# Three order ties in a two-layer diffusion block: a weight sum behind an output add, a cast behind a copy, two subtractions behind a low part

## The chip, the cores and the metric

The kernel runs on one core of one Trainium2 chip. The metric is the device time of one execution in microseconds (us). A core has five engines with instruction queues of their own: TensorE (PE in the profile, with its weight loads shown apart as PEld), VectorE (DVE), ScalarE (ACT), GpSimd (POOL) and SyncE (SP), which here issues most of the loads.

## The reference

Two layers over 512 latent tokens and 256 context tokens of width 1024, batch 1. Layer 0 is windowed attention, layer 1 is retention in both directions; each is followed by a SwiGLU feed-forward of inner width 2816. Only the latent stream is returned. What matters here is layer 1:

```python
def swiglu(h, w_in, w_out):
    gate, up = jnp.split(h @ w_in, 2, axis=-1)
    return (jax.nn.silu(gate) * up) @ w_out

# bidir_retention, 4 heads of 256 (q, k) and 512 (v, g)
q_x, k_x, v_x, g_x = jnp.split(h_x @ w_qkvg, [qk, 2 * qk, 2 * qk + RET_VWIDTH], axis=-1)
ox_f, _ = retention_chunked(q_x, k_x, v_x, log_g[0], state_f)
ox_b, _ = retention_chunked(flip(q_x), flip(k_x), flip(v_x), log_g[1], state_b)
out_x = (jax.nn.silu(g_x) * normed(ox_f + flip(ox_b))) @ w_o

x = x + mx[2] * out_x
x = x + mx[5] * swiglu(modulate(rms_norm(x, norm2_g), mx[3], mx[4]), ffn_w_in, ffn_w_out)
```

All of it is float32.

## The kernel before

**Three products for one.** A float32 operand is split into a rounded high part and the low part that is left: `split` (L164, L165) makes the high part with a cast on ACT and the low part with a subtraction on DVE. A product is then three matmuls: high by high, low by high, high by low (`mm3`, L147 to L149). Each weight tile of 128 x 1024 is loaded by SP into a raw buffer (`w_raw`, L122), split, and used by PE; the raw buffer is loaded again when its low part is done.

**Seven products for eight.** Most projections use Strassen's scheme on quarters of weights and tokens: sums of weight quarters are formed on DVE ahead of the casts, and PE does seven quarter products. The sums accumulate in PSUM, and intermediate sums are copied out by ACT while PE goes on adding to the same bank.

**The retention heads** (loop `for hd in range(RH)`, heads 0 to 3). For value and gate, DVE forms the weight sums `g12` (L1449) and `v11` (L1450), splits `v11` into `w2` (L1451), splits `g12` into `w3`, and, in heads 1 to 3, subtracts `v11` from `v21` (L1456) and splits the result into `w4`. PE uses `w2`, then `w3`, then `w4`, always adding to the banks `Yv` (shown as tile Z); between them ACT copies the sums into `gate` (L1478, L1481). While this goes on, DVE also does the rotary products of the key (`rope_pair`, L1301 to L1303), whose results ACT and DVE split (tiles qk) for the scores.

**The second feed-forward.** The inner width is 22 tiles of 128, in groups of 2, 4, 4, 4, 4, 4. Tiles f = 0 to 2 are plain projections, f = 3 and later use seven products (`seven`, L1727). In each such tile, `quarter_sums` forms four sums in place (L903 to L906): the third, L905, needs the first, L903, and the fourth needs the third. The gate weight and the up weight, as sums, are cast into `b14` and `b32`. PE then does the products Y, Z, Y, X, Y, Z, Y; the third one's running sum is copied out by ACT at L1746, and the fifth product adds to the same bank after that. `output` (L1773) multiplies a finished group with the output weights into two PSUM banks in turn (tile pj), and DVE adds each of the eight output tiles to the residual (`gated_add`, L256). The output of the first group is written in the program after tile f = 2 and ahead of tile f = 3; `first_adds` holds its first two adds. `copies` holds the copies of L1744 and L1746 of the tile before.

**What sets the order.** The program is written in one order; a planner then makes the queue of each engine. It keeps a clock with its own costs, and gives an engine the earliest instruction of the program that is ready by that clock, so that later work can be put ahead of earlier work that isn't ready yet. Data dependences become semaphores. `after(ins, others)` adds an order tie without a semaphore: the planner may not place `ins` before `others`. Each engine then executes its queue in that order.

Of the kernel before, what the change touches and what calls it, by code (L numbers as in the profile page):

```python
# [49 lines left out]
def dit_kernel(ctx, tc, xT, cT, crow, small, consts, masks, tabs0, tabs1, jtab, adaQ, adaN, adaT, wst, out):  # L50
    nc = tc.nc
    mult, add, sub = ALU.mult, ALU.add, ALU.subtract
# [9 lines left out]
    def T(pool, cols, tag, bufs, dt=F32):  # L62
        return pool.tile([P, cols], dt, tag=tag, bufs=bufs, name=tag)
# [27 lines left out]
    def after(ins, others):  # L91
        for o in others:
            tc.add_manual_dep(ins.ins, o.ins.name, order, reason="table set turn")
# [26 lines left out]
    def w_raw(pool=None, bufs=2):  # L120
        raw = T(pool or rp, 1024, "wraw", bufs)
        nc.sync.dma_start(raw, wst[wpos[0]])  # L122
        wpos[0] += 1
        return raw

    def w_parts(pool, own=2):

        bufs = own
        if ring:
            pool, bufs = ring[wsel[0] % len(ring)], 2  # L130
        elif wsel[0] % (2 + own) < 2:
            pool, bufs = rp, 2
        wsel[0] += 1
        return T(pool, 1024, "whi", bufs, F32R), T(pool, 1024, "wlo", bufs, F32R)
# [28 lines left out]
    def split(t, hi, lo, behind=()):  # L163
        after(nc.scalar.copy(hi, t), behind)  # L164
        return nc.vector.tensor_tensor(lo, t, hi, op=sub)  # L165
# [19 lines left out]
    def t_sq(n):  # L185
        return T(rp, 512, "sq", 2)[:, :n]

    def t_hn(n):
        return T(rp, 512, "hn", 2)[:, :n]
# [644 lines left out]
    late = [context[0], latent[0], context[1], latent[1], latent[2], latent[3]]  # L834
# [62 lines left out]
                nc.tensor.matmul(o, p, r, start=first and k + i == 0, stop=k == 3 and i == 2,  # L897
                                 skip_group_check=not first)

    def quarter_sums(g, u, behind=()):  # L900

        l_, r_ = slice(0, 512), slice(512, 1024)
        after(nc.vector.tensor_tensor(g[:, l_], u[:, l_], g[:, l_], op=sub), behind)  # L903
        nc.vector.tensor_tensor(u[:, l_], u[:, r_], u[:, l_], op=sub)
        nc.vector.tensor_tensor(u[:, r_], u[:, r_], g[:, l_], op=sub)  # L905
        nc.vector.tensor_tensor(g[:, r_], g[:, r_], u[:, r_], op=sub)  # L906

    for s in range(2):
# [236 lines left out]
    f, prev = 0, None  # L1145
# [56 lines left out]
    def chunk(i, own=False):  # L1202
        raw = T(qw, 1024, "wx", 4) if own else T(rp, 1024, "wraw", 2)
        nc.sync.dma_start(raw, wst[i])
        return raw

    def split_chunk(raw, behind=()):
        w = w_parts(hpool[0])
        last_split[0] = split(raw, *w, behind)
        return w  # L1210

    last_split, rope_end, rope_sum, hm, other_sums = [None], [None], [None], [], []
# [83 lines left out]
    def rope_pair(o, cos1, sin1, behind=()):  # L1296

        res = []
        for op, f0, f1 in ((sub, cos1, sin1), (add, sin1, cos1)):
            a, b = t_hn(SX), t_sq(SX)  # L1300
            after(nc.vector.tensor_tensor(a, o[0], f0, op=mult), behind)  # L1301
            after(nc.vector.tensor_tensor(b, o[1], f1, op=mult), behind)
            rope_sum[0] = nc.vector.tensor_tensor(a, a, b, op=op)  # L1303
            hi, lo = t_qk(), t_qk()
            rope_end[0] = split(a, hi, lo)
            res.append((hi, lo))
        return res
# [54 lines left out]
    for hd in range(RH):  # L1362
# [28 lines left out]
        for e, o in halves(Y):  # L1391
            nc.scalar.copy(kt[e][:, HALVES[0]], o)
        product_q(X, quarter_of("12"), k21, True)
        later = [nc.vector.tensor_tensor(kt[e][:, HALVES[0]], kt[e][:, HALVES[0]], o, op=add)
                 for e, o in halves(X)]
# [48 lines left out]
        v11 = []  # L1444
        for i in range(2):
# [4 lines left out]
            nc.vector.tensor_tensor(v11[i], g12[i], v11[i], op=add)  # L1450
            w2.append(split_chunk(v11[i]))  # L1451
        if hd:
            w3 = [split_chunk(g) for g in g12]
            for i in range(2):
                v21 = chunk(bv + 2 + i, True)
                nc.vector.tensor_tensor(v21, v21, v11[i], op=sub)  # L1456
                w4.append(split_chunk(v21))
        else:

            ready, w3, lows = last_split[:], [], []  # L1460
            for g in g12:
                w3.append(split_chunk(g))
                lows += last_split
            for i in range(2):
                nc.scalar.activation(v11[i], v11[i], AF.Identity, scale=-1.0)
                nc.gpsimd.dma_start(v11[i], wst[bv + 2 + i], accum_op=add)
            qh = rope_pair(qt, cos1, sin1, ready)
            for low in lows:
                after(low, rope_sum)
# [65 lines left out]
        for i in range(2):  # L1535
            g, v = chunk(bg + i), chunk(bv + i)
# [140 lines left out]
    norm_end, first_end, first_mult, first_adds = [], [], [], []  # L1677
# [49 lines left out]
    def seven(late=()):  # L1727
        g, u = w_raw(fp, 2), w_raw()
        b11 = w_parts(fp, 4)
        b22 = T(hM, 512, "hm", 8, F32R), T(hM, 512, "hm", 8, F32R)  # L1730
        b14, b32 = w_parts(fp, 4), w_parts(fp, 4)
        split(g, *b11, norm_end)
        split(u[:, 512:1024], *b22, norm_end)
        quarter_sums(g, u, first_end[1:2])
        split(u, *b32, first_adds)
        after(split(g, *b14, first_adds), late)
        X, Y, Z = (T(psF, 512, n, 2)[:, 0:SC] for n in "XYZ")
        t, up = t_hn(SX), t_sq(SX)
        e1, e2 = T(rp, 512, "res", 12), T(rp, 512, "res", 12)
        p1, z1, u2, u3 = e1[:, HALVES[0]], e1[:, HALVES[1]], e2[:, HALVES[0]], e2[:, HALVES[1]]  # L1740
        product(Y, operand_a("11"), b11, 0, True)
        act_parts([nc.scalar.copy(p1, Y)])
        product(Z, operand_a(1), b14, 0, True)
        copies[:] = [nc.scalar.copy(z1, Z)]  # L1744
        product(Y, operand_a(2), b32, 512, False)
        copies.append(nc.scalar.copy(u2, Y))  # L1746
        product(X, operand_a("12"), b11, 512, True)
        nc.vector.tensor_tensor(t[:, HALVES[0]], p1, X, op=add)
        silu(t[:, HALVES[0]], t[:, HALVES[0]])
        product(Y, operand_a(3), b32, 0, False)  # L1750
        nc.scalar.copy(u3, Y)
        product(Z, operand_a(4), b22, 0, False)
        nc.vector.tensor_tensor(up[:, HALVES[0]], u2, Z, op=add)
        product(Y, operand_a("22"), b14, 512, False)
        nc.vector.tensor_tensor(up[:, HALVES[1]], u3, z1, op=add)
        silu(t[:, HALVES[1]], Y)
        nc.vector.tensor_tensor(t, t, up, op=mult)
        act = new_act()
        pending.append((t, *act))
        return act  # L1760

    pending, copies, late = [], [], ()

    def act_parts(behind=()):
        ends = []
        while pending:
            t, hi, lo = pending.pop()
            ends.append(nc.scalar.copy(hi, t))
            after(ends[0], behind)
            ends.append(nc.vector.tensor_tensor(lo, t, hi, op=sub))  # L1770
        return ends
# [23 lines left out]
    f, prev = 0, None  # L1795
    for gsz in FFN_GROUPS:
        acts = []
        for i in range(gsz):
# [9 lines left out]
            late = output(prev, False) if i == 0 and prev is not None else ()  # L1808
# [148 lines left out]
```

## Time and profile before

| what | value |
| --- | --- |
| time, median of 3 runs | 1736.23 us (1734.84 to 1737.31) |
| the profiled execution | 1732.25 us |
| its span, first to last instruction | 1730.3 us |
| granted TensorE clock, mean | 0.999 |
| busy PE, PEld | 98%, 87% of the span |
| busy DVE, ACT | 79%, 50% |
| HBM traffic | 117 GB/s mean |
| head 0 of retention | from about 840 us on |
| second feed-forward's first matmuls | about 1390 us |

In a timeline row stand the start in us, the duration in us, the engine, the line, the operation, the tile written and the tiles read, the shapes, the count of merged instructions, and in brackets the idle time ahead of it with what ended it. In a row of waits stand the total in us, the number of waits and the longest. L164 and L165 are the cast and the low part wherever they are called, so the tile names tell which split it is.

### The profile page before, as it was taken

The numbers are of one execution on the slowest core, as the hardware profiler recorded it, in microseconds if no ns is written. First come the engines' busy times: TensorE is split into PE (matmuls) and PEld (weight loads), VectorE is DVE, ScalarE is ACT, GpSimd is POOL, SyncE is SP. The second block draws the span as 40 slices with busy tenths as digits, with TensorE's granted clock in tenths as the row PEclk, the third lists the DMA queues.
The fourth block names the chain that finished last, engine by engine and source line by source line (L and its number), as shares of the span: only waits on it lengthen the run. The fifth ranks groups of instructions, "written<-read, shape, count | busy, mean of one in ns | idle before, by whom it ended". The sixth has DMA issues, their size and how long they took to land.

```text
span 1730.3 us, 27786 instructions
## 1 busy us (share of the span) xinstructions
PE 1698.0 (98%) x10876; PEld 1513.0 (87%) x10876; DVE 1361.0 (79%) x2436; ACT 871.1 (50%) x1552; POOL 50.5 (3%) x168
## 2 busy tenths in 40 slices
PE   7999999999999999999999999999999999999999
PEld 5788877899999999999988788898897899899998
DVE  6698889798778788787889858858758798877874
ACT  5587779465433334342556534524525464445442
POOL 0000000000000000000000000000000000000000
PEclk9999999999999999999999999999999999999999
DMA  9612221543253434343423524523423223333322
GB/s 349 239 30 57 62 62 56 209 134 121 73 157 117 153 110 148 123 154 102 156 99 88 183 77 132 163 82 124 159 90 108 95 74 103 117 102 116 100 86 86
DMA packets 62803, 207.48 MB, mean 120 GB/s; under 512 B 7248, under 2 KB 8912, under 8 KB 62416
## 3 DMA queue, kind: packets, MB, share of 16 engines
q1 hardware_dynamic: 55184, 178.97, 32.0%
q0 software_dynamic: 7200, 26.22, 5.2%
q8 instruction: 85, 1.39, 0.3%
q10 hardware_dynamic: 288, 0.52, 0.1%
q14 instruction: 46, 0.38, 0.1%
HBM read 199.65 MB, written 2.10 MB: 117 GB/s over the span
## 4 chain that ended last, share of the span: by engine, by line
PE 78%; DVE 11%; DMA 6%; ACT 3%; issue 2%; SPq 0%; ACTq 0%; DVEq 0%
PE Y L897 14%; PE pj L147 7%; PE Z L897 7%; PE pj L149 7%; PE pj L148 7%; PE Z L1292 6%; PE X L897 3%; DMA wraw<-in_wst_dram 3%; PE pT L736 2%; PE pO L750 2%; PE S L710 2%; DVE wlo L165 2%; PE Y L1281 2%; PE pj L1292 2%; PE X L1281 1%
## 5 line engine op out<-in xcount | busy, mean ns | idle before, releaser
L164 ACT CAST whi<-wraw 128x1024 fp32r<-128x1024 f32 x258 | 270.0, 1051 | 333.7 <-PE Z L149 81.9
L165 DVE TENSOR_TENSOR wlo<-wraw,whi 128x1024 fp32r<-128x1024 f32 x258 | 314.3, 1221 | 64.5 <-ACT whi L164 62.7
L897 PE MATMUL Y<-aq,whi 128*128 128x384 f32 x640 | 173.5, 335 | 0.6 <-ACT hn L1053 0.6
L897 PEld LDWEIGHTS Y<-aq,whi 128*128 128x128 f32 x640 | 116.6, 188 | 1.6 <-ACT hn L1053 1.4
L256 DVE SCALAR_TENSOR_TENSOR res<-pj,mod,res 128x512 f32<-128x512 f32 (+1 forms) x112 | 81.0, 728 | 41.5 <-PE pj L149 41.2
L897 PE MATMUL Y<-aq,wlo 128*128 128x384 f32 x320 | 107.0, 334 | 0.0
L273 DVE CUSTOM_DVE_ANT_0 y<-adaw,crow,small_sb 128x1024 bf16<-128x1024 f32 x64 | 81.9, 1280 | 29.6 <-DMA adaw<-in_adaT_dram 29.4
L1292 PE MATMUL Z<-whi,sA 128*128 128x512 f32 x256 | 81.7, 394 | 1.4 <-ACT gate L1478 1.4
L101 ACT ACTIVATE pr<-pr,stat,qs 128x513 f32<-128x513 f32 (+2 forms) x96 | 74.2, 775 | 9.1 <-DVE stat L717 8.8
L147 PE MATMUL pj<-ax,whi 128*128 128x512 f32 x176 | 69.0, 392 | 1.2 <-DVE res L256 1.2
L149 PE MATMUL pj<-ax,whi 128*128 128x512 f32 x176 | 68.6, 390 | 0.0
L148 PE MATMUL pj<-ax,wlo 128*128 128x512 f32 x176 | 68.6, 390 | 0.0
L147 PE MATMUL pj<-act,whi 128*128 128x512 f32 x168 | 65.6, 391 | 0.0
L148 PE MATMUL pj<-act,wlo 128*128 128x512 f32 x168 | 65.5, 390 | 0.0
L149 PE MATMUL pj<-act,whi 128*128 128x512 f32 x168 | 65.5, 391 | 0.0
L897 PEld LDWEIGHTS Y<-aq,wlo 128*128 128x128 f32 x320 | 60.1, 188 | 0.0
L1292 PEld LDWEIGHTS Z<-whi,sA 128*128 128x128 f32 x256 | 48.0, 188 | 13.0 <-ACT gate L1478 2.6
L711 DVE CUSTOM_DVE_ANT_0 pr<-S,mask,qs 128x256 f32<-128x256 f32 (+1 forms) x96 | 53.1, 566 | 7.8 <-PE S L710 5.3
L897 PE MATMUL Y<-sA,whi 128*128 128x256 f32 x304 | 58.1, 277 | 0.6 <-ACT res L1746 0.6
L897 PE MATMUL Y<-hx,whi 128*128 128x256 f32 x304 | 56.3, 277 | 0.0
L736 PE MATMUL pT<-const_sb,pr 128*128 128x128 f32 x352 | 53.6, 278 | 1.5 <-ACT tt L738 0.9
L1292 PE MATMUL Z<-wlo,sA 128*128 128x512 f32 x128 | 50.7, 396 | 0.2
(581 smaller groups left out, 5070.4 us busy)
## 6 DMA issues: line engine op xcount, KB each, us to landing
wraw<-in_wst_dram SPq DMA_DIRECT2D x224, 512.0 KB, 3.6
adaw<-in_adaT_dram POOLq DMA_DIRECT2D x48, 512.0 KB, 3.9
wx<-in_wst_dram SPq DMA_DIRECT2D x30, 512.0 KB, 4.3
adan<-in_adaQ_dram SPq DMA_DIRECT2D x16, 512.0 KB, 8.8
adan<-in_adaN_dram SPq DMA_DIRECT2D x12, 512.0 KB, 7.7
adaw<-in_adaT_dram SPq DMA_DIRECT2D x8, 512.0 KB, 3.9
res<-in_xT_dram SPq DMA_DIRECT2D x14, 256.0 KB, 3.2
aq<-in_adaN_dram SPq DMA_DIRECT2D x12, 256.0 KB, 5.7
```

Of the source, the lines that this page charges most:

```text
L101: ins = nc.scalar.activation(*args, **kw)
L147: nc.tensor.matmul(o, whi, xhi, start=first, stop=False)
L148: nc.tensor.matmul(o, wlo, xhi, start=False, stop=False)
L149: return nc.tensor.matmul(o, whi, xlo, start=False, stop=last)
L164: after(nc.scalar.copy(hi, t), behind)
L165: return nc.vector.tensor_tensor(lo, t, hi, op=sub)
L256: return nc.vector.scalar_tensor_tensor(res[d], o, mods[l, s][:, part, d:d + 1], res[d], mult, add)
L273: res.append(nc.vector.tensor_tensor_reduce(junk, w, cr[:, s * 1024:(s + 1) * 1024], 1.0, sm_t[:, C_ADAB + l * 48 + j:C_ADAB + l * 48 + j ...
L711: nc.vector.tensor_tensor_reduce(pt[:, c0:c0 + w], bank, mask[:, m0:m0 + w], 1.0, top, add, ALU.min, lo)
L736: nc.tensor.transpose(tp[:, a * P:(a + 1) * P], self.pr[(0, 2, 1, 3)[a]][:, ki * P:(ki + 1) * P], ident)
L897: nc.tensor.matmul(o, p, r, start=first and k + i == 0, stop=k == 3 and i == 2, skip_group_check=not first)
L1292: ins = nc.tensor.matmul(os[t], p, r, start=first and k + i == 0, stop=k == 3 and i == 2, skip_group_check=by_k or not first)
```

## The change

Three order ties are added; no instruction is added, removed or altered.

1. In `quarter_sums`, the third sum (L905, DVE) gets an optional list `later`, and `seven` passes the first output add (`first_adds[:1]`, DVE). For tile f = 3 this add is the one of the output written just ahead; for the later tiles it lies far back.
2. In tile f = 5, the cast of `b14` (ACT) is tied behind `copies[1]`, the copy of L1746 of tile f = 4 (ACT).
3. In heads 1 to 3, the two subtractions of L1456 (DVE) are tied behind the low part of the second `w2` tile (DVE).

```diff
-    def quarter_sums(g, u, behind=()):
+    def quarter_sums(g, u, behind=(), later=()):
         l_, r_ = slice(0, 512), slice(512, 1024)
         after(nc.vector.tensor_tensor(g[:, l_], u[:, l_], g[:, l_], op=sub), behind)
         nc.vector.tensor_tensor(u[:, l_], u[:, r_], u[:, l_], op=sub)
-        nc.vector.tensor_tensor(u[:, r_], u[:, r_], g[:, l_], op=sub)
+        after(nc.vector.tensor_tensor(u[:, r_], u[:, r_], g[:, l_], op=sub), later)
         nc.vector.tensor_tensor(g[:, r_], g[:, r_], u[:, r_], op=sub)
...
         if hd:
+            ready = last_split[:]
             w3 = [split_chunk(g) for g in g12]
             for i in range(2):
                 v21 = chunk(bv + 2 + i, True)
-                nc.vector.tensor_tensor(v21, v21, v11[i], op=sub)
+                after(nc.vector.tensor_tensor(v21, v21, v11[i], op=sub), ready)
                 w4.append(split_chunk(v21))
...
-        quarter_sums(g, u, first_end[1:2])
+        quarter_sums(g, u, first_end[1:2], first_adds[:1])
         split(u, *b32, first_adds)
-        after(split(g, *b14, first_adds), late)
+        after(split(g, *b14, first_adds + (copies[1:2] if f == 5 else [])), late)
```

## The prediction

> **What bounds the kernel now.** I read the page's busy rows first, then the waits of TensorE (PE) and of its weight loads (PEld) where the change lies, then the timeline engine by engine.
>
> ```profile
> PE 1698.0 (98%) x10876; PEld 1513.0 (87%) x10876; DVE 1361.0 (79%) x2436; ACT 871.1 (50%) x1552; POOL 50.5 (3%) x168
> ```
>
> The page: PE is the bound in every stage, so an edit is worth only the PE time that it frees. The waits of PE from 1400 us on (waiting line, releaser, us in total, times, longest):
>
> ```profile
> PE pj L147 <- DVE res L256: 1.2, 2, 1.0
> PE Y L897 <- ACT res L1746: 0.6, 1, 0.6
> ```
>
> The waits of PEld from 1045 to 1335 us, retention heads 1 to 3, where the same view of PE lists none:
>
> ```profile
> PEld Z L1292 <- DVE wlo L165: 1.5, 3, 0.6
> PEld Z L1292 <- ACT gate L1478: 0.8, 3, 0.3
> ```
>
> So there are three places, each on a line that the change touches or just behind it. PE's idle column understates them: a matmul's row reaches into the next one (0.39 us long, 0.23 us apart), so I price each stall by the distance between starts. The Trainium skill, Perfetto Trace Analysis, section Identifying the Most-Contended Engine, says that matmul busy time is a poor measure because matmuls are pipelined, and that the weight loads' is better. By the idle column the three places would be worth 1.0 + 0.6 + 0 = 1.6 us and the time 1734.6; the PEld rows above show that here the page is right.
>
> **Nothing is added or removed.** Every tie is between two instructions of one engine (sum and add on DVE, cast and copy on ACT, subtraction and low part on DVE), carries no semaphore, and only sets the order in which the planner writes that engine's queue. Busy time, traffic and the number of semaphore waits should stay; the ties of `later` for tiles after the fourth are met long before and cost nothing.
>
> **Part 1, the weight sum behind the first output add.** DVE, then PE, timeline of before:
>
> ```profile
> 1422.93 0.68 DVE L905 TENSOR_TENSOR wraw<-wraw 128x512 f32<-128x512 f32 x1
> 1423.64 0.69 DVE L906 TENSOR_TENSOR wraw<-wraw 128x512 f32<-128x512 f32 x1
> 1424.25 1.40 DVE L256 SCALAR_TENSOR_TENSOR res<-pj,mod,res 128x512 f32<-128x512 f32 x2
> 1425.57 0.68 DVE L1707 TENSOR_TENSOR hn<-hn,Y 128x512 f32<-128x512 f32 x1
> 1426.74 0.75 DVE L256 SCALAR_TENSOR_TENSOR res<-pj,mod,res 128x512 f32<-128x512 f32 x1 [0.50 <-PE pj L149]
> 1427.41 1.22 DVE L165 TENSOR_TENSOR wlo<-wraw,whi 128x1024 fp32r<-128x1024 f32 x1
> ...
> 1429.14 1.41 DVE L256 SCALAR_TENSOR_TENSOR res<-pj,mod,res 128x512 f32<-128x512 f32 x2
> ```
>
> ```profile
> 1422.33 0.39 PE L149 MATMUL pj<-ax,whi 128*128 128x512 f32 x1
> ...
> 1423.69 0.39 PE L149 MATMUL pj<-ax,whi 128*128 128x512 f32 x1
> 1425.05 0.50 PE L147 MATMUL pj<-ax,whi 128*128 128x512 f32 x1 [0.97 <-DVE res L256]
> 1425.39 0.40 PE L148 MATMUL pj<-ax,wlo 128*128 128x512 f32 x1
> ```
>
> Output tile 0 is complete at 1422.33 + 0.39 = 1422.72, but its add (L256) stands behind L905 and L906 and starts at 1424.25; output tile 2 needs the bank that this add frees. Its second matmul starts at 1425.39, where an unbroken row gives 1423.69 + 2 x 0.23 = 1424.15: the stall costs 1.24 us.
>
> Tied, the add takes L905's place at 1422.93 and ends at about 1423.65, before tile 2's turn at 1423.92. L905 moves to 1423.6. Late next is the second add: if L906 is still ahead of it, it starts at 1424.8 and ends at 1425.55, where tile 3 wants the other bank at 1423.92 + 6 x 0.23 = 1425.30, a new wait of 0.25 us. Further on DVE is nearly full: from 1422.93 to the fourth add at 1429.14 it idles 0.50 us and 0.1 more, so that add can come only 0.6 us earlier unless the planner puts a low part behind it. Bounds: 0.6 (DVE's slack, same order) and 1.24 (the whole stall); I take 0.9. Behind L905 in its own chain wait the fourth tile's two casts on ACT; their low part at 1427.41 would start some 0.7 us later at worst, and its product comes after the five or six output tiles that are left, at 1.37 us each, so nobody waits.
>
> **Part 2, the cast behind the running sum's copy.** ACT, then PE with the same product of the next tile for comparison (1457.89 and 1460.61):
>
> ```profile
> 1446.86 1.05 ACT L164 CAST whi<-wraw 128x1024 fp32r<-128x1024 f32 x1 [0.29 <-DVE wraw L905]
> 1448.06 1.05 ACT L164 CAST whi<-wraw 128x1024 fp32r<-128x1024 f32 x1 [0.15 <-DVE wraw L906]
> 1449.01 0.36 ACT L1746 COPY res<-Y 128x256 f32<-128x256 f32 x1
> 1449.28 1.05 ACT L164 CAST whi<-wraw 128x1024 fp32r<-128x1024 f32 x1
> ```
>
> ```profile
> 1447.24 0.28 PE L897 MATMUL Y<-sA,whi 128*128 128x256 f32 x1
> 1447.35 0.28 PE L897 MATMUL X<-hx,whi 128*128 128x256 f32 x1
> ...
> 1450.95 0.28 PE L897 MATMUL Z<-sA,hm 128*128 128x256 f32 x1
> ...
> 1457.89 0.28 PE L897 MATMUL X<-hx,whi 128*128 128x256 f32 x1
> ...
> 1460.61 1.52 PE L897 MATMUL Z<-sA,hm 128*128 128x256 f32 x12
> ```
>
> The sum in Y is complete at 1447.52; its copy waits for two casts. From X's first matmul to Z's PE needs 3.60 us here and 2.72 us one tile later: the stall costs 0.88 us. Tied, the second cast (b14 of f = 5) goes behind the copy. The copy then starts where the first cast leaves ACT, 1447.8, and ends at 1448.2; PE wants it at 1447.35 + 1.37 = 1448.72. The cast starts at 1448.1 instead of 1448.06, since it was waiting for L906: it costs nothing. If the first cast doesn't move forward with PE's 0.9 us of part 1, PE wants the copy at 1447.8 and waits 0.4 us. Bounds 0.45 and 0.88; the first cast hangs on a DVE chain that follows PE, so I take 0.8. The next cast (1449.28, b11 of f = 6) can't take the gap in its stead: its buffers are those of f = 4's b11, which the X product still reads.
>
> **Part 3, two subtractions behind a low part, heads 1 to 3.** The rows of head 1, the other two have the same order. DVE, then ACT, then PE:
>
> ```profile
> 1057.11 0.68 DVE L165 TENSOR_TENSOR qk<-hn,qk 128x512 fp32r<-128x512 f32 x1
> ...
> 1058.31 1.22 DVE L1450 TENSOR_TENSOR wraw<-wx,wraw 128x1024 f32<-128x1024 f32 x1
> 1059.45 2.35 DVE L1456 TENSOR_TENSOR wx<-wx,wraw 128x1024 f32<-128x1024 f32 x2
> 1061.72 1.21 DVE L165 TENSOR_TENSOR wlo<-wraw,whi 128x1024 fp32r<-128x1024 f32 x1
> ...
> 1063.99 0.68 DVE L1301 TENSOR_TENSOR hn<-gate,rj 128x512 f32<-128x512 f32 x1
> ...
> 1066.93 0.68 DVE L1303 TENSOR_TENSOR hn<-hn,sq 128x512 f32<-128x512 f32 x1
> ```
>
> ```profile
> 1059.62 1.06 ACT L164 CAST whi<-wraw 128x1024 fp32r<-128x1024 f32 x1 [3.42 <-DVE wraw L1450]
> ...
> 1067.65 0.63 ACT L164 CAST qk<-hn 128x512 fp32r<-128x512 f32 x1 [0.76 <-DVE hn L1303]
> 1068.18 1.04 ACT L164 CAST whi<-wx 128x1024 fp32r<-128x1024 f32 x1
> 1069.12 0.58 ACT L1478 COPY gate<-Z 128x512 f32<-128x512 f32 x1
> ```
>
> ```profile
> 1062.33 0.62 PE L1292 MATMUL Z<-whi,sA 128*128 128x512 f32 x2
> ...
> 1063.33 0.63 PE L1292 MATMUL Z<-whi,sA 128*128 128x512 f32 x2
> ...
> 1069.53 0.73 PE L1292 MATMUL Z<-whi,sA 128*128 128x512 f32 x2
> 1070.09 0.39 PE L1292 MATMUL Z<-wlo,sA 128*128 128x512 f32 x1
> ```
>
> The low part of w2 could start when its cast ends, 1059.62 + 1.06 = 1060.68, but the two subtractions hold DVE until 1061.72. PE pays 1063.33 - (1062.33 + 3 x 0.23) = 0.31 us. Six microseconds on, a gate copy that is late on ACT costs 1070.09 - (1069.53 + 2 x 0.23) = 0.10 us. Three heads: 0.93 + 0.30 = 1.23 us. The PEld rows give 1.5 + 0.8 = 2.3 us as the upper end.
>
> Two things decide whether PE keeps this. First, what fills DVE from 1059.45 to 1060.68. The rotary products of the key (L1301, then L1302) read tiles that are complete, and the last reader of their two scratch buffers is the low part at 1057.11; two of them at 0.60 us (0.68 less the overlap with the next) fit exactly. Second, the gate copy: PE comes 0.31 us earlier to it, and if it stays at 1069.12 it takes the 0.31 us back. Its queue is held by the qk cast, which waits for L1303. With two rotary products done early, L1303 stands behind L1450, two products, three low parts and two subtractions, 1058.31 + 1.14 + 1.2 + 5 x 1.14 = 1066.35, so 0.6 us earlier, and the copy with it. The subtractions then end by about 1066.4 in the worst order; the second of the two casts that read them is the row at 1068.18, and their product is the one after the w3 product, so their delay reaches nobody. Bounds: 2.3 and, with DVE idle in the gap, below nothing (rival D). I take 1.2, nearest to the starts.
>
> **The sum.** 0.9 + 0.8 + 1.2 = 2.9 us. The profiled execution took 1732.25 us (span 1730.3), which is 4.0 us under the median 1736.23 of the three runs; it would become 1729.35, the median 1733.3. That is 0.17%; about 0.2% (3.5 us) is what a measurement of this kernel can tell from no change.
>
> **The rivals.**
> - B, the stalls were dearer than their starts show: 1.24 + 0.88 + 2.3 = 4.4 us, and up to 5.2 if the DVE queue, moved forward, also shortens the small waits behind it. 1731.8 to 1731.0. For it: PEld's rows. Against: PE's starts.
> - C, the gate copy doesn't move: each head gives its gain back at L1478, and 1.7 us are left: 1734.5. For it: ACT's order there is tight, 1067.65 to 1069.70 without a gap.
> - D, slower: the planner leaves DVE idle in the gap. 1.2 us of hole shift L1303 to 1068.1 and the copy to 1070.3; PE, which went on at 1069.86, loses 1.2 us in each head, 3.6 in all, less 1.7 from the feed-forward: +1.9, 1738.1. It decides from a copy 0.57 us late (1.7 / 3). Against it: L1301 was chosen by the planner between two low parts, so it was ready and waiting.
> - E, slower by more: the planner's clock moves and it reorders work that isn't tied, a weight load above all. A load takes
>
> ```profile
> wraw<-in_wst_dram SPq DMA_DIRECT2D x224, 512.0 KB, 3.6
> ```
>
> 3.6 us to land; two exposed ones less the 2.9 give +4.3, 1740.5. Nothing in the rows speaks for it, except that the ties do change what the planner sees.
>
> **The chances.** My forecast A (2.2 to 3.9 us gained, 1732.3 to 1734.0) has 0.48, of which 0.20 lies beyond the 3.5 us; B 0.18, C 0.13, D 0.11, of which 0.02 loses over 3.5 us because part 1 fails too; E 0.10. Faster by over 0.2%: 0.20 + 0.18 = 0.38. Within: 0.28 + 0.13 + 0.09 = 0.50. Slower: 0.02 + 0.10 = 0.12. The range 1731.0 to 1738.0 goes from B's far end to D and leaves E out.
>
> **What would show it.** Part 1: L256 at about 1422.9, L905 behind it, and no 0.97 on L147. Part 2: L1746 between the two casts and 2.7 us from X to Z. Part 3: L1301 or L1302 ahead of the low part, no PEld wait on wlo, and the gate copy at least 0.4 us earlier. Wrong it would be by an idle gap on DVE ahead of that low part, by a new wait on L1478, or by weight loads in another order.

## The result, and the profile after

| | median | runs | against before of the same session (95%) |
| --- | --- | --- | --- |
| before | 1734.7 us | 22 | |
| after | 1732.13 us | 22 | 0.9987 (0.9981 to 0.9993): -2.3 us (-3.3 to -1.2) |
| after, on another chip later | 1732.43 us | 11 | 0.9983 (0.9974 to 0.9992): -2.9 us (-4.5 to -1.4) |

The change makes the kernel a little faster, by less than the 0.2% that the prediction called tellable. The forecast was 1733.3 us and a gain of 2.9 us. The size is right, but by the traces the gain comes from the second feed-forward alone; the third part's did not arrive as forecast, as follows. All microseconds below that stand beside a ratio are that ratio times the median of before in its session.

The three places of the prediction first. Page and waits of TensorE from 1400 us on, kernel after:

```profile
PE 1700.0 (98%) x10876; PEld 1515.2 (88%) x10876; DVE 1361.1 (79%) x2436; ACT 870.4 (50%) x1552; POOL 50.4 (3%) x168
```

```profile
PE pj L147 <- DVE res L256: 0.4, 1, 0.4
```

The 1.2 us on L256 are down to 0.4, and the row of L897 is gone from this view. VectorE and ScalarE do the work they did before, so nothing was bought with extra work. PE's busy time is 2 us higher in the kernel that is no slower, so it prices nothing here.

The first output tiles, kernel after, timeline of VectorE and then of TensorE:

```profile
1422.56 0.68 DVE L904 TENSOR_TENSOR wraw<-wraw 128x512 f32<-128x512 f32 x1
1423.16 0.68 DVE L165 TENSOR_TENSOR hm<-wraw,hm 128x512 fp32r<-128x512 f32 x1
1423.77 0.74 DVE L256 SCALAR_TENSOR_TENSOR res<-pj,mod,res 128x512 f32<-128x512 f32 x1
1424.43 0.68 DVE L905 TENSOR_TENSOR wraw<-wraw 128x512 f32<-128x512 f32 x1
1425.03 0.74 DVE L256 SCALAR_TENSOR_TENSOR res<-pj,mod,res 128x512 f32<-128x512 f32 x1
...
1426.94 0.68 DVE L906 TENSOR_TENSOR wraw<-wraw 128x512 f32<-128x512 f32 x1
...
1428.30 0.74 DVE L256 SCALAR_TENSOR_TENSOR res<-pj,mod,res 128x512 f32<-128x512 f32 x1
1428.96 1.21 DVE L165 TENSOR_TENSOR wlo<-wraw,whi 128x1024 fp32r<-128x1024 f32 x1
```

```profile
1424.40 0.39 PE L149 MATMUL pj<-ax,whi 128*128 128x512 f32 x1
1424.62 0.44 PE L147 MATMUL pj<-ax,whi 128*128 128x512 f32 x1
1424.90 0.40 PE L148 MATMUL pj<-ax,wlo 128*128 128x512 f32 x1
```

L905 now stands behind the first add, L906 behind the third and the low part of the weight (wlo) behind the fourth, and output tile 2 follows tile 1 with no break: its second matmul starts at 1424.90, where 1424.40 + 2 x 0.23 = 1424.86 is unbroken. The stall of 1.24 us is down to 0.04.

The cast and the copy, kernel after, ScalarE and then TensorE:

```profile
1447.38 1.05 ACT L164 CAST whi<-wraw 128x1024 fp32r<-128x1024 f32 x1 [1.05 <-DVE wraw L905]
1448.34 0.36 ACT L1747 COPY res<-Y 128x256 f32<-128x256 f32 x1
1448.60 2.01 ACT L164 CAST whi<-wraw 128x1024 fp32r<-128x1024 f32 x2
```

```profile
1447.12 0.28 PE L897 MATMUL X<-hx,whi 128*128 128x256 f32 x1
...
1450.23 1.52 PE L897 MATMUL Z<-sA,hm 128*128 128x256 f32 x12
```

The copy (now L1747) stands between the casts as forecast. From X to Z TensorE takes 3.11 us instead of 3.60; the unbroken 2.72 are not reached, because the first cast, still ahead of the copy, waited 1.05 us for L905 and did not come forward.

Head 1 of the retention, kernel after, VectorE:

```profile
1058.02 1.22 DVE L1450 TENSOR_TENSOR wraw<-wx,wraw 128x1024 f32<-128x1024 f32 x1
1059.15 0.68 DVE L1301 TENSOR_TENSOR hn<-gate,rj 128x512 f32<-128x512 f32 x1
1059.75 0.68 DVE L1302 TENSOR_TENSOR sq<-gate,rj 128x512 f32<-128x512 f32 x1
1060.40 1.23 DVE L165 TENSOR_TENSOR wlo<-wraw,whi 128x1024 fp32r<-128x1024 f32 x1
1061.54 1.22 DVE L1457 TENSOR_TENSOR wx<-wx,wraw 128x1024 f32<-128x1024 f32 x1
```

Just the order that the prediction worked out: two rotary products fill the gap, the low part comes 1.32 us earlier, the subtraction (now L1457) behind it. Now the waits over heads 1 to 3, 1045 to 1335 us, weight loads and then matmuls, kernel after:

```profile
PEld X L1522 <- DVE wx L165: 4.1, 5, 1.3
PEld Z L1292 <- ACT gate L1479: 0.5, 1, 0.5
```

```profile
PE X L1522 <- DVE wx L165: 1.9, 4, 0.9
```

The row on wlo is gone. In its place stands a row that the prediction does not speak of, X waiting for wx. X is the bank that sums score times value, and the tile wx here holds the high and low parts of a score. The row was in the kernel before as well, and led the very view from which the prediction took two rows:

```profile
PEld X L1521 <- DVE wx L165: 2.1, 5, 0.5
```

It has doubled, and matmuls, not only weight loads, now wait there. One profile of each kernel would be little to go by, but the later runs agree: the four profiles with part 3 and no tie at the scores (the next section has them) have 4.0 to 4.6 us in this row, the four with neither 2.0 to 3.2. This is what the experiments had to explain.

### The profile page after: what moved, and what is told of

It reads as the page before. It is cut to its first block, busy times and chain, and to the rows that moved or that the text cites. A ratio compares the mean times of both kernels' runs of the same rounds, so it can differ in the third digit from the quotient of the medians.

```text
span 1729.8 us, 27790 instructions
## 1 busy us (share of the span) xinstructions
PE 1700.0 (98%) x10876; PEld 1515.2 (88%) x10876; DVE 1361.1 (79%) x2436; ACT 870.4 (50%) x1552; POOL 50.4 (3%) x168
## 4 chain that ended last, share of the span: by engine, by line
PE 79%; DVE 12%; DMA 5%; ACT 2%; issue 2%; SPq 0%; DVEq 0%; ACTq 0%
PE Y L897 15%; PE Z L897 8%; PE pj L147 7%; PE pj L149 7%; PE pj L148 7%; PE X L897 4%; DMA wraw<-in_wst_dram 4%; PE Z L1292 4%; DVE wlo L165 3%; PE pT L736 2%; PE pO L750 2%; PE S L710 2%; PE X L149 1%; PE X L147 1%; PE X L148 1%
## 5 line engine op out<-in xcount | busy, mean ns | idle before, releaser
L897 PE MATMUL Y<-aq,whi 128*128 128x384 f32 x640 | 173.7, 335 | 0.0
L897 PEld LDWEIGHTS Y<-aq,whi 128*128 128x128 f32 x640 | 116.6, 188 | 1.1 <-ACT hn L1053 1.1
L256 DVE SCALAR_TENSOR_TENSOR res<-pj,mod,res 128x512 f32<-128x512 f32 (+1 forms) x112 | 81.0, 728 | 39.4 <-PE pj L149 39.2
L897 PE MATMUL Y<-aq,wlo 128*128 128x384 f32 x320 | 107.0, 334 | 0.0
L897 PEld LDWEIGHTS Y<-aq,wlo 128*128 128x128 f32 x320 | 60.1, 188 | 0.0
L897 PE MATMUL Y<-sA,whi 128*128 128x256 f32 x304 | 58.1, 277 | 0.1
L897 PE MATMUL Y<-hx,whi 128*128 128x256 f32 x304 | 56.3, 277 | 0.0
L736 PEld LDWEIGHTS pT<-const_sb,pr 128*128 128x128 f32 x352 | 40.2, 142 | 12.0 <-issue 4.0
```

What stands on the lines that cost most here:

```text
L256: return nc.vector.scalar_tensor_tensor(res[d], o, mods[l, s][:, part, d:d + 1], res[d], mult, add)
L736: nc.tensor.transpose(tp[:, a * P:(a + 1) * P], self.pr[(0, 2, 1, 3)[a]][:, ki * P:(ki + 1) * P], ident)
```

## The experiments

Two numbers are used throughout. One is the ratio above, which for most runs is known to some 1.5 us either way. The other is a balance from the traces: TensorE's n-th matmul in a run against its n-th in the profile of before, each from its own start, once ahead of and once behind a stage; the change of that lag is what the stage cost (+) or gained (-). Heads 1 to 3 are measured between the matmuls at 1042.0 and 1379.7 us of before, the second feed-forward between those at 1419.8 and 1725.5.

| kernel | parts of the change | further tie | ratio (95%) | heads 1-3, us | second feed-forward, us |
| --- | --- | --- | --- | --- | --- |
| before | none | | 1 | 0 | 0 |
| retention only | 3 | | 0.9999 (0.9990 to 1.0008) | +0.93 | +1.63 |
| feed-forward only | 1, 2 | | 0.9996 (0.9987 to 1.0005) | +0.81 | -0.66 |
| sum only | 1 | | 0.9989 (0.9980 to 0.9998) | -0.13 | -1.00 |
| cast only | 2 | | 0.9997 (0.9988 to 1.0006) | +0.53 | +0.20 |
| after, its two runs | 1, 2, 3 | | 0.9987, 0.9983 | +0.76, +1.21 | -1.20, -1.64 |
| tie alone | none | scores | 0.9982 (0.9973 to 0.9990) | -2.01 | +0.58 |
| parts 1, 2 and tie | 1, 2 | scores | 0.9967 (0.9955 to 0.9980) | -1.02 | -0.61 |
| after and tie | 1, 2, 3 | scores | 0.9957 (0.9944 to 0.9971) | -1.46 | -1.17 |
| the same again | 1, 2, 3 | scores | 0.9959 (0.9947 to 0.9972) | -2.59 | -2.54 |
| tie at the second score | 1, 2, 3 | scores, later | 0.9972 (0.9961 to 0.9984) | -2.50 | -1.34 |
| sum behind two adds | 1, 2, 3 | feed-forward | 1.0017 (1.0008 to 1.0026) | +0.53 | +3.50 |
| both ties | 1, 2, 3 | both | 0.9993 (0.9984 to 1.0002) | -2.87 | +4.25 |

Two profiles of one kernel differ by 0.4 to 1.4 us in a stage, so single figures of the last two columns say little, groups of them more. The profile of before, the zero of both columns, was itself 2.4 us under its median.

Two rows of the table are one program by their profiles. In those of "feed-forward only" and "sum only" every engine does the same operations in the same order from start to end. So their ratios, 0.9996 and 0.9989, and their stages, 0.9 us apart in heads 1 to 3, differ by chance, and part 2's tie changes nothing where part 1's is present. From 1380 us on that same order stands in the changed kernel too, and in each kernel with parts 1 and 2 and no further tie in the feed-forward.

### The parts one by one

Part 3 alone is the kernel before with this:

```diff
+            ready = last_split[:]
             w3 = [split_chunk(g) for g in g12]
...
-                nc.vector.tensor_tensor(v21, v21, v11[i], op=sub)
+                after(nc.vector.tensor_tensor(v21, v21, v11[i], op=sub), ready)
```

> The kernel before with the third part of the change alone (the two subtractions of heads 1 to 3 tied behind the low part). Theory of the forecast: the 1.2 us of part 3 arrive at the end, 1733.5 against 1734.7 (-1.2 us). Rival theory, give-back: in the trace of the changed kernel TensorE is 0.34 to 0.42 us ahead after the two wlo steps of a head and loses 0.29 to 0.82 us again at the scores (L1521, L1522), because the low part of the first score stands on VectorE behind a weight sum that waits for its load, and that load follows VectorE's work and not TensorE's. Then this kernel is at 1734.7 +-0.5 us (0), with TensorE ahead of the kernel before by less than 0.3 us at the end of head 3, while its waits on wlo in heads 1 to 3 are gone all the same (3 waits, 1.5 us before, 0 here).

Measured: -0.2 us (-1.7 to +1.4). By time alone neither theory is excluded. The trace decides for the give-back: the wait on wlo is gone, TensorE gains 0.34, 0.42 and 0.30 us at the wlo steps of the three heads and some more at two of the three gate copies, and it loses 0.63, 0.69 and 0.77 us at their scores. Its waits from 1045 to 1335 us, matmuls:

```profile
PE X L1522 <- DVE wx L165: 2.2, 4, 0.8
```

The predicted gains are there and are lost again; the balance of heads 1 to 3 is +0.93 us. The mean of the three profiles with part 3 and no tie is +0.97, of the four without either (before, feed-forward only, sum only, cast only) +0.30. The places say it more clearly. At the three wlo steps together TensorE gains 1.03 to 1.06 us in each of the eight profiles with part 3, against -0.91 to +0.40 in the six without. At the three heads' scores it loses 1.9 to 2.5 us in the four with part 3 and no tie there, against -0.2 to +1.3 in the four with neither.

Parts 1 and 2 alone, which is the diff of the change without the lines above:

> The kernel before with the first and second part alone (the weight sum of the second feed-forward behind the first output add, the cast behind the copy). Theory of the forecast: 0.9 + 0.8 = 1.7 us, 1733.0 against 1734.7. Rival theory, give-back in the retention: the whole gain of the change, 2.3 us, is these two parts, 1732.4. Both have the wait on L256 ahead of the matmuls of L147 and the wait of L897 on the res cast gone.

Measured: -0.7 us (-2.3 to +0.9), 1733.22 us by the median: less than either theory asks for, with an interval that reaches both. Its waits on the res cast and the first wait on L256 are gone as expected of both, and TensorE gains 1.27 and 0.52 us at the two places. Over the whole stage the eight profiles with this order (both parts or part 1, no further tie in the feed-forward) stand at -1.27 us on average, the three with neither (before, retention only, tie alone) at +0.74: the new order is worth some 2 us by the trace.

Part 1 alone:

```diff
-        quarter_sums(g, u, first_end[1:2])
+        quarter_sums(g, u, first_end[1:2], first_adds[:1])
```

> The first part alone: the third instruction of the weight sums (L905) behind the first output add. Forecast: -0.9 us (0.6 to 1.24), 1733.8 against 1734.7. Rival: TensorE's starts in the changed kernel are 1.18 us earlier at the second tile, 0.80 us earlier at the outputs of the next group, and later by 0.20, 0.20 and 0.71 us at three further outputs where L903 waits for its load ahead of L256; if all of these come from this edit, it is worth 0.2 to 1.3 us, with the places of the later losses the same.

Measured: -1.9 us (-3.5 to -0.3), beyond the rival's 0.2 to 1.3, with an interval that reaches down to the forecast. TensorE is 1.27 us ahead at output tile 2. One of the three later losses is there (0.31 us, the second group); the other two are in the kernel with part 2 alone (0.20 and 0.54 us), so they do not belong to this edit.

What neither theory says: part 1 alone also brings part 2's gain, 0.52 us at the same place. ScalarE in this kernel, without part 2's tie:

```profile
1446.02 1.05 ACT L164 CAST whi<-wraw 128x1024 fp32r<-128x1024 f32 x1 [0.97 <-DVE wraw L905]
1446.98 0.36 ACT L1746 COPY res<-Y 128x256 f32<-128x256 f32 x1
```

The planner, whose clock part 1 moves, puts the copy between the two casts by itself. So this run measures both places and not part 1 alone. With the run before it, the same program, it gives -0.7 and -1.9 us, some 1.3 us for the feed-forward edit as a whole.

Part 2 alone:

```diff
-        after(split(g, *b14, first_adds), late)
+        after(split(g, *b14, first_adds + (copies[1:2] if f == 5 else [])), late)
```

> The second part alone: the cast on ScalarE in the sixth tile of the second feed-forward behind the second copy of the running sum. Forecast: -0.8 us (0.45 to 0.88), 1733.9 against 1734.7. Rival: TensorE starts 0.48 us earlier there in the changed kernel, and the next group's outputs stand behind a weight sum L903 that waits for its load; if that load does not move, the gain is lost there and this kernel is at 1734.7 +-0.4 us, with a longer wait on L256 at the next group in its place.

Measured: -0.5 us (-2.1 to +1.0), which tells the two apart as little. The place itself, ScalarE in this kernel:

```profile
1448.00 1.06 ACT L164 CAST whi<-wraw 128x1024 fp32r<-128x1024 f32 x1 [0.44 <-DVE wraw L905]
1448.96 0.37 ACT L1746 COPY res<-Y 128x256 f32<-128x256 f32 x1
```

The cast ahead of the copy waits for L905 here too, without part 1. TensorE gains 0.54 us at the place (0.48 in the changed kernel), not 0.88, and loses 0.80 us again one tile later, where it waits for another copy of ScalarE (L1742, one wait of 0.5 us). The loss expected at the next group did not come: there it gains. Two other kernels keep the order of before here, retention only and the tie alone; from X to Z they take 4.37 and 4.13 us where before took 3.60, so the stall that this tie removes varies between profiles from 0.88 to 1.65 us.

### The scores: where part 3's gain goes

The chain in head 1 of the kernel after, VectorE, the load that it waits for, and TensorE:

```profile
1071.97 1.22 DVE L1538 TENSOR_TENSOR wraw<-wraw 128x1024 f32<-128x1024 f32 x1
...
1074.37 1.23 DVE L165 TENSOR_TENSOR wlo<-wraw,whi 128x1024 fp32r<-128x1024 f32 x1 [0.57 <-ACT whi L164]
...
1079.32 1.22 DVE L1538 TENSOR_TENSOR wraw<-wraw 128x1024 f32<-128x1024 f32 x1 [2.20 <-DMA wraw<-in_wst_dram]
1080.46 0.68 DVE L165 TENSOR_TENSOR wx<-hn,wx 128x512 fp32r<-128x512 f32 x1
```

```profile
1075.62 0.33 SPq L1204 DMA_DIRECT2D wraw<-in_wst_dram  x1
```

```profile
1080.57 0.39 PE L1521 MATMUL X<-wx 128*128 128x512 f32 x1
1081.20 0.50 PE L1522 MATMUL X<-wx 128*128 128x512 f32 x1 [0.25 <-DVE wx L165]
```

Read it upwards. X waits for the low part of the first score, `wx<-hn` at 1080.46. That low part stands on VectorE behind the second weight sum of the next product (L1538), which itself waited 2.20 us for a load. The load was issued at 1075.62, when the low part at 1074.37 had ended and freed one of the two wraw buffers, and that goes back to the first sum at 1071.97. From 1061.54 to that sum VectorE had been busy without a gap. So the moment at which X may go on is set by VectorE's work and a load of some 3.7 us, and not by TensorE: a TensorE that arrives earlier waits longer. Before, VectorE's same rows stood at 1079.60 and 1080.75:

```profile
1079.60 1.22 DVE L1537 TENSOR_TENSOR wraw<-wraw 128x1024 f32<-128x1024 f32 x1 [1.98 <-DMA wraw<-in_wst_dram]
1080.75 0.68 DVE L165 TENSOR_TENSOR wx<-hn,wx 128x512 fp32r<-128x512 f32 x1
```

```profile
1081.06 0.39 PE L1520 MATMUL X<-wx 128*128 128x512 f32 x1
1081.48 0.50 PE L1521 MATMUL X<-wx 128*128 128x512 f32 x1
1081.82 0.40 PE L1519 MATMUL X<-wx 128*128 128x512 f32 x1
```

TensorE arrives 0.49 us earlier after the change (1080.57 against 1081.06), VectorE's low part only 0.29 us, and the rest, 0.20, is lost at the spot. The Trainium skill, PSUM — Partial Sum Buffer, section Engine vs sequencer instructions, states that VectorE's queue is strictly first in, first out. The trace agrees: the low part's own cast on ScalarE was done at 1077.83, and still the low part went only when the waiting sum ahead of it had. ScalarE, kernel after:

```profile
1077.21 0.62 ACT L164 CAST wx<-hn 128x512 fp32r<-128x512 f32 x1 [1.57 <-DVE hn L1512]
```

If so, taking the sum out of the way must return the gain. The tie, on top of the change, for heads 1 to 3:

```diff
-            split(sd, ss[:, 0:512], ss[:, 512:])
+            score_lows.append(split(sd, ss[:, 0:512], ss[:, 512:]))
...
-            after(nc.vector.tensor_tensor(g, g, v, op=sub), [] if hd else rope_end)
+            after(nc.vector.tensor_tensor(g, g, v, op=sub), (score_lows[:1] if i else []) if hd else rope_end)
```

> The changed kernel with one more tie: in heads 1 to 3 the second g-minus-v weight sum (L1538) stands behind the low part of the first score on VectorE, so that its wait for its load no longer holds that low part up. Give-back theory: TensorE's wait at L1522 for the low part (1.9 us, 4 in the changed kernel) goes to under 0.6 us, the loss of 0.2 to 0.8 us per head at the first score goes, and over the stretch of heads 1 to 3 TensorE gains 0.5 to 1.5 us where the changed kernel loses 0.9; the end comes 1 to 2 us earlier than the changed kernel's, near 1731. Rival: the sum comes about 1.1 us later, with it the cast of the weight behind it, and the gap moves to the matmuls that read this weight; then the time is that of the changed kernel, with a wait on whi or wlo in place of the one on wx.

Measured: -7.5 us (-9.7 to -5.0) against before, 1727.76 us by the median, some 4 to 5 us under the changed kernel and so more than the theory asked for. Because that was much and the runs were few, it was run again beside the changed kernel on one chip:

> The changed kernel once more, beside the next three on one chip: 2.3 us under the kernel before, as measured (1.2 to 3.3). All theories agree; it is the base for the other three.

> The changed kernel with the tie at the scores once more (6.6 us under the kernel before with 5 runs). Give-back theory: 3 to 4.5 us under the changed kernel of this call. If the first time was a chance of few runs, 1 to 2 us under it.

Measured: -2.9 us for the changed kernel, -7.1 us (-9.2 to -4.9) with the tie, 1728.82 against 1732.43 us by the medians. The give-back theory holds. The same place in this second run, VectorE and TensorE:

```profile
1078.28 0.69 DVE L165 TENSOR_TENSOR wx<-hn,wx 128x512 fp32r<-128x512 f32 x1 [0.74 <-ACT wx L164]
...
1080.28 1.23 DVE L1539 TENSOR_TENSOR wraw<-wraw 128x1024 f32<-128x1024 f32 x1 [0.70 <-DMA wraw<-in_wst_dram]
```

```profile
1080.98 0.39 PE L1521 MATMUL X<-wx 128*128 128x512 f32 x1
1081.21 0.39 PE L1522 MATMUL X<-wx 128*128 128x512 f32 x1
```

The low part is out 2 us before X wants it, the sum (L1539 in this kernel) waits only 0.70 us for its load, and TensorE runs at 0.23 us a matmul. The weight loads' wait on wx over heads 1 to 3, 4.1 us after the change, is down to one of 0.2:

```profile
PEld Z L1292 <- ACT gate L1479: 0.7, 1, 0.7
PEld Z L1292 <- DVE wlo L165: 0.2, 1, 0.2
PEld X L1522 <- DVE wx L165: 0.2, 1, 0.2
```

Does the tie need part 3? The tie alone on the kernel before:

> The kernel before with the tie at the scores alone, without the three parts of the change. Give-back theory: TensorE keeps its idle at the wlo steps (the wait of weight loads on wlo, 3 times, 1.5 us), and its rhythm is set by VectorE's loads and sums; there is no wait at L1521 in heads 1 to 3 of the kernel before (only weight loads that wait 2.1 us), so the tie alone gains little: 0 to 0.8 us. If it gains as much as the changed kernel with the tie does over the changed kernel, the low part at the scores is a cost of its own, independent of part 3.

Measured: -3.1 us (-4.7 to -1.7), against 0 to 0.8 expected: a miss. The low part behind the loading sum was a cost of its own before the change, and by the medians no smaller than what all three parts of the change bring (the intervals overlap). As expected the wait on wlo stays:

```profile
PEld Z L1292 <- DVE wlo L165: 1.4, 3, 0.8
```

At the scores TensorE gains 0.37, 0.33, 0.39, 0.15, 0.37 and 0.31 us at the first and the third score of the three heads, 1.9 us in all, where the view of TensorE's own waits lists nothing in the kernel before. In five of the six profiles with the tie the three heads together gain 1.6 to 1.9 us there; in the sixth, the first run on top of the change, one wait of 1.0 us in head 3 leaves 0.4.

And is part 3 worth its forecast once the tie is there? Parts 1 and 2 with the tie:

> The first and second part and the tie at the scores, without the third part. It shows what part 3 is worth when its gain is no longer handed back at the scores. Theory: part 3 then brings the 1.2 us of the forecast (0.34 to 0.56 us per head at the wlo steps), so this kernel is 1.2 us (0.7 to 1.7) slower than the one with all three parts and the tie. Rival: part 3 brings nothing even then, since VectorE's work sets the pace of heads 1 to 3; this kernel's time is that of the one with all parts, within 0.4 us.

Measured: -5.7 us (-7.8 to -3.5), 1.2 us slower than all three parts with the tie by the medians (1730.03 against 1728.82), as forecast; the intervals overlap, so the time alone does not exclude the rival. The waits show the mechanism. The weight loads from 1045 to 1335 us in this kernel:

```profile
PEld Z L1292 <- DVE wlo L165: 2.4, 3, 1.1
```

Without part 3 the wait on wlo stays, with the tie (1.4 and 2.4 us) as without it (0.9 to 1.7); with part 3 it is 0.2 at most in all eight profiles, and the 1.03 to 1.06 us at the wlo steps are kept once the scores no longer take them. So part 3 needs the tie to pay; the tie does not need part 3, as the run before showed.

A tie one score later:

```diff
-            after(nc.vector.tensor_tensor(g, g, v, op=sub), (score_lows[:1] if i else []) if hd else rope_end)
+            after(nc.vector.tensor_tensor(g, g, v, op=sub), (score_lows[1:2] if i else []) if hd else rope_end)
```

> The changed kernel with the second weight sum (L1538) of heads 1 to 3 behind the low part of the second score instead of the first. In the first run with the tie TensorE lost 0.97 us in head 3 at the second score, whose low part stood behind that sum. Theory: this loss goes and the end comes 0 to 1 us earlier than with the tie at the first score. Rival: the sum now comes some 4 us later, and so do the cast and the low part of this weight and the loads of the two weights behind it; the matmuls that read them wait, and the end comes 1 us later or more.

Measured: -4.9 us (-6.8 to -2.8), 2.7 us slower by the medians than the first tie beside it, which is the rival's side; but the intervals overlap, heads 1 to 3 stand at -2.50 us, no better and no worse than the -1.46 and -2.59 of the first tie, and no matmul there waits for a weight. The loss of 0.97 us in head 3 that this edit was to remove is absent in the second run of the first tie as well, so it was no fixed cost of that tie. Nor do the 2.7 us show at the tie: in its profiled execution this kernel was 2.80 us behind the profile of before already at 1042 us, ahead of head 1, and 2.25 of them at 60 us, where the order of work is the same in both. The kernel with the first tie was 0.24 us ahead at 1042. No run shows whether the other executions were late there too.

### The feed-forward: the first sum behind the second add

L903 still waits for its load ahead of an L256, in four groups of output tiles in the profile of the changed kernel (3.1 us in all). Tied behind the second add:

```diff
-        quarter_sums(g, u, first_end[1:2], first_adds[:1])
+        quarter_sums(g, u, first_end[1:2] + list(late[1:2]), first_adds[:1])
...
-        after(split(g, *b14, first_adds + (copies[1:2] if f == 5 else [])), late)
+        after(split(g, *b14, first_adds + (copies[1:2] if f == 5 else [])), late[3:4])
...
-        return adds[3:4]
+        return adds
```

The line of `b14` is changed only so that its tie stays behind the fourth add, now that `output` returns all adds.

> The changed kernel with one more tie: in the second feed-forward the first weight sum of a tile (L903), which waits for its load ahead of the output add L256 in three groups, stands behind the second output add. If that load wait is what costs the outputs, TensorE's losses of 0.20, 0.20 and 0.71 us at the later groups' outputs go, the waits of L147 on L256 (0.4 us in the changed kernel, 1.0 to 1.2 us without the first part) go to 0, and the end comes 0.5 to 1.1 us earlier. Rival: the sums and the cast behind them come later than TensorE needs them, and waits of L897 on the cast weight take their place: no gain, or up to 1 us slower.

Measured: 1.0017, +2.9 us (+1.4 to +4.5) against before and 5 us slower than the changed kernel: the rival's sign was right, its size too small, and the waits are not where it put them. Waits of TensorE from 1345 us on, and VectorE at the first of the later groups:

```profile
PE pj L147 <- DVE res L256: 2.3, 4, 0.6
PE Y L897 <- ACT res L1752: 1.1, 2, 0.8
```

```profile
1485.10 0.68 DVE L905 TENSOR_TENSOR wraw<-wraw 128x512 f32<-128x512 f32 x1
1485.82 0.69 DVE L906 TENSOR_TENSOR wraw<-wraw 128x512 f32<-128x512 f32 x1
1486.97 1.23 DVE L165 TENSOR_TENSOR wlo<-wraw,whi 128x1024 fp32r<-128x1024 f32 x1 [0.47 <-ACT whi L164]
1488.12 0.74 DVE L256 SCALAR_TENSOR_TENSOR res<-pj,mod,res 128x512 f32<-128x512 f32 x1
```

The wait of L903 is not removed but handed on: the sums that start later now stand, with a low part that waits for its cast, ahead of the fourth add of the same group. Against the kernel before, TensorE loses 0.84 to 0.94 us this way at one place in each of four groups.

Both ties together:

> Both further ties on top of the change. If both theories hold their gains add, since the stages follow one another: 1.5 to 3 us under the changed kernel, 3.5 to 5.5 us under the kernel before (ratio 0.997 to 0.998). If only the first holds, 1 to 2 us under the changed kernel; if neither, its time.

Measured: -1.2 us (-2.8 to +0.3). The stages do add: -2.87 us in heads 1 to 3 and +4.25 in the feed-forward. The kernel that beats both is the changed one with the tie at the scores, 0.9957 and 0.9959 of before.

## Why the prediction was right, and where not

- **The time.** Forecast -2.9 us, measured -2.3 (-3.3 to -1.2) and -2.9. Over 22 runs the median of before was 1734.7 us, not the 1736.23 of the first three, which moved the absolute time by 1.5 us: 1733.3 forecast, 1732.13 measured. So the time fell into the range, and the gain into the band of 2.2 to 3.9 us of forecast A, but not by the forecast's own sum.
- **Part 1, 0.9 taken between 0.6 and 1.24.** Mechanism right, size at the upper end: 1.18 to 1.27 us at output tile 2. The term that was mis-sized is "that add can come only 0.6 us earlier", the slack of VectorE in the old order. The prediction added "unless the planner puts a low part behind it", and that is what happened: L906 went behind the third add and the low part behind the fourth, which starts at 1428.30 instead of 1429.14. In the first profile 0.17 us is lost again by 1434 us; in the seven others with the same order at most 0.02 is. The wait of 0.25 us feared at tile 3 did not come.
- **Part 2, 0.8 taken between 0.45 and 0.88.** Here the lower end was true: 0.48 to 0.54 us. The prediction had named the condition (the first cast doesn't come forward, and TensorE waits 0.4 us: it measured 3.11 - 2.72 = 0.39) and then chose against it. The step that failed is "the first cast hangs on a DVE chain that follows PE". The cast waited 1.05 us for L905, and VectorE was busy without a gap from 1441.65 until L905 began at 1446.66: the chain followed VectorE's own queue. A second step failed that the prediction did not see. It took the two places as two edits whose gains add; the order that this tie asks for comes out of part 1 alone. The tie is needed only without part 1. And the 0.88 us were the smallest stall of the three profiles that keep this order.
- **Part 3, 1.2 us.** The local steps held, all but one: two rotary products in the gap, the wait on wlo gone, gains of 0.30 to 0.42 us per head at wlo against 0.31, and of 0.12 to 0.14 at the gate copy in heads 1 and 2 against 0.10, the copy 0.84 us earlier in head 1 against 0.6. In head 3 of the first profile the gate copy came late instead and cost 0.20 us, the sign of rival C; the second profile of the same kernel gains 0.11 there. What failed is "Two things decide whether PE keeps this". There is a third, 18 us on, and it has the form of rival C, a gain handed back in each head, at another line: L1521 and its wx in place of L1478 and its gate copy. The forecast's own window listed that row, and above the two rows quoted. That its gain is taken back at the scores is shown by the traces: 1.06 us won at wlo, some 1.8 us more lost at the scores than without part 3 (means of four profiles each). The time of part 3 alone (-0.2 us, -1.7 to +1.4) agrees with a part that is worth nothing and does not prove it.
- **That the sum came out is in good part luck.** Part 3's 1.2 us of it did not arrive, and the feed-forward gave more than the 1.7 us set down for it: some 2 us by the balance, 1.18 to 1.27 us at the first place and about 0.5 at the second against the smallest stall there. By the balance the whole change would be worth 1.3 to 1.4 us, a gain of 2.0 less 0.6 to 0.7 in the heads; the time says 2.3 (1.2 to 3.3), and what makes up the rest is not shown. The separately measured parts (-0.2 us, and -0.7 and -1.9 for the two runs of the feed-forward edit) agree with either within their intervals.
- **Rivals.** B: only part 1 came up to its term, 1.24 us; the later profiles suggest that part 2's stall was dearer than the rows of before show. C: its handing back came, but at the scores. D: VectorE did not idle in the gap. E: the loads' order on SyncE is the same.
- **Still open.** The tie at the scores moves the time by about 4 us on top of the change, and there the matmuls' starts agree: 1.9 to 2.5 us lost at the scores without it, 1.6 to 1.9 gained with it in all but one profile. Alone it moves the time by 3.1 us (1.7 to 4.7), while the starts show 1.9 us against the profile of before and 2.3 against the mean of the four without part 3 and tie; that profile was 2.4 us under its median, which may be the rest. No run leaves out part 2 alone, so that it is idle in the full change rests on the equal order of the feed-forward. Taking the load's wait away by a buffer of its own was not tried.

## What to carry to other kernels

When an edit makes the bounding engine arrive earlier, follow it forward to the next place that another engine sets by its own clock, and read whether the thing waited for moves as well; here it was a row of the same view. Before a gain is put down to one of several ties, compare the order that each kernel really runs: one tie can move the planner so that another has nothing left to do. On an engine that works through its queue in order, look for an instruction that waits for a load and at what stands behind it: a short one that the bounding engine needs should go ahead of it, and the price is whatever then stands behind the sum instead, which was next to nothing at the scores and more than the gain in the feed-forward, where the kernel became 5 us slower. A wait that shows on weight loads alone can still cost time, as the 2.1 us on wx did here.

## What the runs showed of the hardware

After a matmul that waited, the next one follows late as well. In the kernel before the third X matmul starts at 1081.48, 0.19 us later than 1081.06 + 0.23, with no wait in its row at all; the wait stands on its weight load, 0.45 us. The next one starts 0.34 us after it instead of 0.23, and the lag settles at 0.37 us, which is what the tie alone gives back there. The same 0.34 stands between 1425.05 and 1425.39, at the first feed-forward stall, and between 1081.20 and the next start at 1081.54 after the change. So in these three cases a stall cost 0.1 to 0.2 us more than its apparent delay, which doubled the one of 0.19 us, and TensorE's own waits show a part of it or none: 0.97 of 1.24 us at the first feed-forward stall, nothing of the 0.37. The Trainium skill, Perfetto Trace Analysis, section Identifying the Most-Contended Engine, says that the matmuls' busy share is not a good measure of how close a kernel is to what the engine can do, and gives the weight loads' busy share as one of two to use instead. It speaks of busy shares; for waits this trace shows the like: 2.1 us on the weight loads, none on the matmuls, and 1.9 us gained when the cause was taken away.
